# Ordering the block products' preparations on VectorE in one of two feed-forward parts

## The chip, the cores and the metric

The kernel runs on one core of one Trainium2 chip. The metric is device time in microseconds (us), median of several runs; a profiled execution is a run of its own with the hardware profiler on.

## The reference

One decoder layer in float32, x of 512 tokens by 1024 features:

```
x = x + 0.5 * rms_norm(swiglu(rms_norm(x, ffn1_pre), ffn1 weights), ffn1_post)
x = x + rms_norm(token_mixer(rms_norm(x, mix_pre)), mix_post)
x = x + 0.5 * rms_norm(swiglu(rms_norm(x, ffn2_pre), ffn2 weights), ffn2_post)
swiglu(h) = (silu(h @ w_gate) * (h @ w_up)) @ w_down        # w_gate, w_up: 1024 x 2816
```

The token mixer (sparse and dilated attention) stands between the two feed-forward parts and isn't touched.

## The kernel before, in words

**Precision.** Each float32 operand is split into a high half (a cast to fp32r, on ScalarE, line 139) and a low half (source minus high half, on VectorE, line 140). A product then takes three matmuls: high by high, high by low, low by high (`mm3`, lines 162 to 164). For a weight the halves are the tiles whi and wlo, three buffers each. In a product the third matmul is the first that reads wlo. `split` keeps its latest VectorE instruction in `self.last_sub`.

**Block products.** The 2816 hidden features are 22 tiles of 128, taken as 11 pairs p of an even and an odd block. Pairs 0 and 1 are computed plainly. For the pairs 2 to 10 gate and up projections go by a seven-product scheme of the Strassen kind: instead of eight products of block by token half there are seven, P1 to P7, on sums of weight blocks and on sums of token halves made before. Each product has 24 matmuls of 128x128 by 256 tokens, into one bank of PSUM. The seven are run in the order P2, P6, P5, P7, the next pair's P1, P4, P3.

**Preparations.** `prep` makes a product's weight ready: for P6 two sums of raw blocks (lines 509, 510) and one more sum in place (line 524), for P3 one difference in place (line 521), and for every product `entry`, a cast and a subtraction over 128x1024 (lines 139, 140, tiles whi and wlo). P6 and P5 read the sums, tiles tmp; the others read raw blocks. When a raw block is done with, `refill` sends the next load into it through SyncE's queue (line 331; lines 525 and 527 call it). The loop at lines 570 to 581 prepares `AHEAD` = 2 products ahead: in one turn it calls `prep` for the product after next, then `run` for the current one, then `finished`.

**After a product.** `finished` takes results out of PSUM: ScalarE copies (line 544), VectorE adds (lines 548, 553, 560), and `swiglu` (activation on ScalarE at line 402, product on VectorE at line 403; in the first part also a scaling at line 401). Behind P3 `sums` makes sums of the pair's even and odd activations for the down projection, which goes by the same scheme (lines 409 to 412), stores some of them (lines 414 to 419), and for the pairs below `later` splits the even half into fp32r halves at once (lines 423, 424). `later` is 3 in the first part and 11 in the second, so the first part splits there in pairs 0 to 2 and the second in all.

**What sets the order.** A planner puts each engine's instructions in an order when the kernel is built: by its own estimates of time it takes what is ready, the earlier written first, and it may pull later work into a gap. Semaphores and buffers are derived from that. `issue_after(ins)` adds order edges: every instruction that is traced inside the block and belongs to the engine of `ins` is placed behind `ins`. Such an edge is on one engine and needs no semaphore. Around `prep` it is given `self.last_sub`, an instruction of VectorE; so ScalarE's casts and SyncE's refills have no edge of it. `self.last_sub` is whatever split was traced last, be it that of the preparation before or, behind P3, the one in `sums`.

**The two parts.** Both are the function `ffn`. The first is called with `opened`, a dictionary of what the kernel's opening has made; in the second call `opened` is None. The first part also computes weight sums for the down projection by accumulating DMAs (`weight_sums`) during the block products.

Of the kernel before, what the change touches and what calls it, by code (L numbers as in the profile page):

```python
# [61 lines left out]
class Layer:  # L62
# [274 lines left out]
    def ffn(self, gu, wd, td, post, finish, xsrc, aside=None, opened=None):  # L337
# [163 lines left out]
        def prep(p, name):  # L501
            st = state.setdefault(p, {})
            if name == "P1":
                src = blk(p, 0, 0)
            elif name == "P2":
                src = blk(p, 1, 0)
            elif name == "P6":
                s1, s2 = [self.sbt("tmp", [P, D], bufs=2) for _ in range(2)]
                nc.vector.tensor_add(s1, blk(p, 0, 1), blk(p, 1, 1))
                nc.vector.tensor_sub(s2, s1, blk(p, 0, 0))  # L510
                st["s"] = s1, s2
                src = s2
            elif name == "P5":
                src = st["s"][0]
            elif name == "P7":
                src = blk(p, 0, 1)
            elif name == "P4":
                src = blk(p, 1, 1)
            else:
                src = blk(p, 1, 0)  # L520
                nc.vector.tensor_sub(src, src, st["s"][1])
            st[name] = entry(src)
            if name == "P6":
                nc.vector.tensor_sub(blk(p, 0, 1), blk(p, 0, 0), blk(p, 0, 1))
                self.refill(blk(p, 0, 0))
            elif name in ("P7", "P4", "P3"):
                self.refill(src)

        def run(p, name):
            st = state[p]  # L530
            w = st.pop(name)
            bank, top = dict(P1="XB11", P2="YB21", P6="XT2", P5="ZT1", P7="XT3", P4="XT4", P3="ZB22")[name][0:1], \
                dict(P1="B11", P2="B21", P6="T2", P5="T1", P7="T3", P4="T4", P3="B22")[name]
            start = name in ("P1", "P2", "P5")
            if start:
                st[bank] = self.bank()
            product(w, top, st[bank], start)

        def finished(p, name):
            st = state[p]  # L540
            t0, t1 = slice(0, 256), slice(256, 512)
            if name in ("P1", "P6", "P7"):
                v = self.slot("V")
                nc.scalar.copy(v, st["X"])
                st[name + "c"] = v
            if name == "P2":
                v = st["P1c"]
                nc.vector.tensor_add(v, st["Y"], v)
                st["ev"] = self.slot(LATER_TAGS[0][p - later] if p >= later else "ring")
                st["od"] = self.slot("W")  # L550
                swiglu(st["ev"][:, t0], v[:, t0], v[:, t1], t0)
            elif name == "P7":
                nc.vector.tensor_add(v, st["Z"], v)
                swiglu(st["od"][:, t1], v[:, t0], v[:, t1], t1)
            elif name == "P4":
                b = st["X"]
                swiglu(st["od"][:, t0], b[:, t0], b[:, t1], t0)
            elif name == "P3":
                v = st["P6c"]
                nc.vector.tensor_add(v, st["Z"], v)  # L560
                swiglu(st["ev"][:, t1], v[:, t0], v[:, t1], t1)
                sums(p, st["ev"], st["od"])
                extra(p)
                del state[p]
# [4 lines left out]
        done, first = 0, {}  # L569
        for i, (p, name) in enumerate(todo):  # L570
            while done < len(todo) and done <= i + AHEAD:
                with self.tc.issue_after(self.last_sub) if done else ExitStack():
                    prep(*todo[done])
                done += 1
            run(p, name)
            if p == NP - 1 and name in ("P4", "P3"):
                k0 = 2 * len(first)
                r = self.blocks_of.pop(("B11", k0))
                first[k0] = self.wsplit(r.rearrange("p (k d) -> p k d", d=S), [2, S])
                self.refill(r)  # L580
            finished(p, name)
# [1173 lines left out]
```

## Time and profile before

| what | value |
|---|---|
| median of 3 runs | 1138.02 us (1136.74 to 1138.59) |
| the profiled execution's own time | 1144.58 us |
| its span | 1142.8 us |
| TensorE busy | 1106.7 us (97%) |
| VectorE busy | 885.5 us (77%) |
| ScalarE busy | 643.0 us (56%) |
| DMA, mean over the span | 199 GB/s |
| block products of the second part, from and to | 843.5 to 1029.3 us |

How to read it: the profile names engines PE (TensorE matmuls), PEld (its weight loads), DVE (VectorE), ACT (ScalarE), POOL (GpSimd), SP (SyncE). L140 is line 140 of the kernel. A group or a row gives line, engine, operation, and output tile <- input tiles. In a timeline a row begins with its start and its duration in us, and what stands in square brackets is the idle time of the engine before it and the instruction that ended it. Tiles named pb_S, pb_T, pb_F, pb_V are banks of PSUM; xhl_t and SP_s hold the halves of the tokens and of their sums.

### The profile page before, as it was taken

Reading aid. Unit: us, or ns where it says so; the run is one execution under the profiler, and the core shown is the slowest. Engines: PE = TensorE matmul, PEld = TensorE weight load, DVE = VectorE, ACT = ScalarE, POOL = GpSimd, SP = SyncE. Lnnn points to the kernel's source line nnn. Section 1 sums busy time; section 2 is a strip of 40 time slices with the busy share of each in tenths; the row PEclk is TensorE's granted clock in tenths of the full one; section 3 lists DMA queues with packets and bytes.
Section 4 is the critical chain, followed back from the end, with each engine's and each line's share of the span. In section 5 each row is a group of like instructions: output and inputs, shape, how many; then the busy total and the mean of one; then the engine's idle time right before and its main releaser. Section 6 shows DMA issues by size and latency. Waiting matters only on the chain.

```text
span 1142.8 us, 18548 instructions
## 1 busy us (share of the span) xinstructions
PE 1106.7 (97%) x6863; PEld 983.2 (86%) x6863; DVE 885.5 (77%) x1554; ACT 643.0 (56%) x1151; POOL 195.5 (17%) x264
## 2 busy tenths in 40 slices
PE   8999999999999999999999999999999999999997
PEld 7899999977888887777888898888989899887886
DVE  6888999977787889787454656977878989889665
ACT  7454555556574778676564635644435545548452
POOL 0334455420011046553000000001000000000000
PEclk9999999999999999999999999999999999999999
DMA  9699999999973589993224426482234433369863
GB/s 353 208 269 274 295 297 260 292 322 311 319 213 98 183 242 285 276 256 85 82 83 130 133 73 175 139 312 95 77 115 134 130 125 119 122 196 296 292 187 106
DMA packets 115594, 227.53 MB, mean 199 GB/s; under 512 B 21904, under 2 KB 51632, under 8 KB 115504
## 3 DMA queue, kind: packets, MB, share of 16 engines
q1 hardware_dynamic: 99136, 174.18, 46.7%
q0 software_dynamic: 16224, 51.91, 18.2%
q8 instruction: 54, 0.88, 0.3%
q14 instruction: 36, 0.29, 0.1%
q10 hardware_dynamic: 144, 0.26, 0.1%
HBM read 191.66 MB, written 57.72 MB: 218 GB/s over the span
## 4 chain that ended last, share of the span: by engine, by line
PE 72%; DVE 10%; DMA 8%; ACT 4%; issue 4%; POOL 1%; SPq 1%; DVEq 0%; POOLq 0%; ACTq 0%
PE pb_F L164 8%; PE pb_F L163 8%; PE pb_F L162 8%; PE pb_S L164 7%; PE pb_S L163 7%; PE pb_S L162 7%; PE pb_T L164 5%; PE pb_T L163 5%; PE pb_T L162 5%; DMA tdram<-in_d_dram 4%; DVE wlo L140 3%; PE pb_V L162 2%; PE pb_V L163 2%; PE pb_V L164 2%; DMA SP_s<-odram 2%
## 5 line engine op out<-in xcount | busy, mean ns | idle before, releaser
L140 DVE TENSOR_TENSOR wlo<-raw,whi 128x1024 fp32r<-128x1024 f32 (+2 forms) x224 | 264.5, 1186 | 142.1 <-ACT whi L139 137.5
L139 ACT CAST whi<-raw 128x1024 fp32r<-128x1024 f32 (+2 forms) x224 | 228.0, 1020 | 201.9 <-PE pb_F L163 57.0
L162 PE MATMUL pb_F<-xhl_t,whi 128*128 128x512 f32 (+1 forms) x440 | 155.4, 353 | 2.0 <-DVE Q_s L1387 1.2
L164 PE MATMUL pb_F<-xhl_t,wlo 128*128 128x512 f32 (+1 forms) x440 | 154.4, 351 | 0.5 <-DVE wlo L140 0.5
L163 PE MATMUL pb_F<-xhl_t,whi 128*128 128x512 f32 (+1 forms) x440 | 154.3, 351 | 0.0
L183 POOL TENSOR_TENSOR rs_t<-rs_t,mhalf_t 128x1 f32<-128x1 f32 x20 | 13.2, 659 | 571.6 <-DVE rs_t L179 571.6
L162 PEld LDWEIGHTS pb_F<-xhl_t,whi 128*128 128x128 f32 x440 | 82.8, 188 | 12.4 <-DVE Q_s L1387 1.4
L164 PEld LDWEIGHTS pb_F<-xhl_t,wlo 128*128 128x128 f32 x440 | 83.1, 189 | 10.9 <-DVE wlo L140 1.2
L163 PEld LDWEIGHTS pb_F<-xhl_t,whi 128*128 128x128 f32 x440 | 83.0, 189 | 9.6 <-issue 0.2
L162 PE MATMUL pb_S<-xhl_t,whi 128*128 128x256 f32 (+1 forms) x280 | 84.0, 300 | 1.5 <-ACT whi L139 0.8
L163 PE MATMUL pb_S<-xhl_t,whi 128*128 128x256 f32 (+1 forms) x280 | 83.7, 299 | 0.0
L164 PE MATMUL pb_S<-xhl_t,wlo 128*128 128x256 f32 (+1 forms) x280 | 83.5, 299 | 0.0
L1136 POOL TENSOR_SCALAR SP_s<-SP_s,st_t 128x384 f32<-128x384 f32 (+2 forms) x48 | 48.5, 1080 | 72.5 <-DMA raw<-in_w_in_dram 48.7
L162 PEld LDWEIGHTS pb_S<-xhl_t,whi 128*128 128x128 f32 x280 | 52.6, 188 | 4.1 <-ACT whi L139 1.0
L162 PE MATMUL pb_T<-xhl_t,whi 128*128 128x256 f32 x200 | 55.7, 279 | 0.0
L163 PE MATMUL pb_T<-xhl_t,whi 128*128 128x256 f32 x200 | 55.7, 278 | 0.0
L164 PE MATMUL pb_T<-xhl_t,wlo 128*128 128x256 f32 x200 | 55.7, 278 | 0.0
L164 PEld LDWEIGHTS pb_S<-xhl_t,wlo 128*128 128x128 f32 x280 | 53.0, 189 | 2.2
L163 PEld LDWEIGHTS pb_S<-xhl_t,whi 128*128 128x128 f32 x280 | 52.7, 188 | 2.2
L139 ACT CAST whi<-tmp_t 128x1024 fp32r<-128x1024 f32 x36 | 36.3, 1051 | 27.0 <-DVE tmp_t L510 24.0
L164 PE MATMUL pb_S<-SP_s,wlo 128*128 128x256 f32 x160 | 44.9, 281 | 3.8 <-DVE wlo L140 3.8
L140 DVE TENSOR_TENSOR PT_s<-pb_T,PT_s 128x512 fp32r<-128x512 f32 (+1 forms) x72 | 39.3, 560 | 7.1 <-ACT PT_s L139 6.5
(849 smaller groups left out, 3325.7 us busy)
## 6 DMA issues: line engine op xcount, KB each, us to landing
raw<-in_gu_dram SPq DMA_DIRECT2D x74, 512.0 KB, 4.3
raw<-tdram SPq DMA_DIRECT2D x40, 512.0 KB, 5.2
raw<-in_w_in_dram SPq DMA_DIRECT2D x18, 1024.0 KB, 5.3
PT_s<-in_d_dram POOLq DMA_DIRECT2D x66, 256.0 KB, 6.8
raw<-in_d_dram SPq DMA_DIRECT2D x30, 512.0 KB, 4.8
tdram<-in_d_dram POOLq DMA_DIRECT2D x18, 768.0 KB, 11.3
tdram<-PT_s POOLq DMA_DIRECT2D x44, 256.0 KB, 5.5
odram<-W_s SPq DMA_DIRECT2D x22, 256.0 KB, 4.5
```

What stands on the lines that cost most here:

```text
L139: self.last_cast = self.nc.scalar.copy(dsthi, src).ins
L140: self.last_sub = self.nc.vector.tensor_sub(dstlo, src, dsthi.bitcast(F32)).ins
L162: mm(out, lhi, rhi, start=start, stop=False, skip_group_check=skip)
L163: mm(out, lhi, rlo, start=False, stop=False, skip_group_check=skip)
L164: mm(out, llo, rhi, start=False, stop=stop, skip_group_check=skip)
L183: nc.gpsimd.tensor_tensor(out=r, in0=v, in1=self.mhalf, op=OP.pow)
L1136: self.last_pool = nc.gpsimd.tensor_scalar(pp, pp, st[:, 1, t:t + 1], None, op0=OP.mult).ins
```

## The change

The edge around `prep` is set in the first feed-forward part alone. `opened` is a dictionary there and None in the second part, where from now on every preparation is traced without an edge.

```
         for i, (p, name) in enumerate(todo):
             while done < len(todo) and done <= i + AHEAD:
-                with self.tc.issue_after(self.last_sub) if done else ExitStack():
+                with self.tc.issue_after(self.last_sub) if done and opened else ExitStack():
                     prep(*todo[done])
                 done += 1
             run(p, name)
```

More of the change, by code (lines that the diff above doesn't have):

```diff
@@ L571, in ffn @@
             while done < len(todo) and done <= i + AHEAD:
-                with self.tc.issue_after(self.last_sub) if done else ExitStack():
+                with self.tc.issue_after(self.last_sub) if done and opened else ExitStack():
                     prep(*todo[done])
```

## The prediction

> **What bounds the kernel now.** I read the page first, for the engine that sets the time.
>
> ```profile
> span 1142.8 us, 18548 instructions
> PE 1106.7 (97%) x6863; PEld 983.2 (86%) x6863; DVE 885.5 (77%) x1554; ACT 643.0 (56%) x1151; POOL 195.5 (17%) x264
> ```
>
> TensorE (PE) is the bound nearly everywhere, so a reordering on VectorE (DVE) can pay only where TensorE waits for it. Next comes the view by windows. I laid it over one pair of feature blocks (seven products) in the first feed-forward part and over one in the second; its columns are stretch and length, then busy time and instructions of PE, PEld, DVE, ACT and POOL, the granted clock, the DMA share and GB/s.
>
> ```profile
> 150.05:169.84 19.79, 19.79 (x171) 19.79 (x169) 18.50 (x26) 10.42 (x14) 9.66 (x12) 1.00 0.96 278
> 862.50:883.10 20.60, 19.32 (x171) 19.12 (x170) 18.17 (x24) 10.77 (x15) 0.00 (x0) 1.00 0.43 135
> ```
>
> In the first part TensorE is busy for the whole pair. In the second it idles 1.28 us, at the same clock and with fewer DMAs. The view of waits between 840 and 1030 us names who is waited for (total, times, longest):
>
> ```profile
> PE pb_S L164 <- DVE wlo L140: 3.8, 3, 1.3
> PE pb_F L164 <- DVE wlo L140: 2.6, 2, 1.3
> PE pb_T L164 <- DVE wlo L140: 2.6, 2, 1.3
> PE pb_V L164 <- DVE wlo L140: 1.3, 1, 1.3
> ```
>
> That is eight waits, 3+2+2+1, one for each of the pairs 3 to 10, all for the low half (wlo) that line 140 makes on VectorE. The chain that ended last goes through these subtractions:
>
> ```profile
> 871.06 1.23 DVE wlo L140
> ...
> 994.66 1.23 DVE wlo L140
> ```
>
> Six pairs lie between these two, (994.66 - 871.06)/6 = 20.60 us each. Now one such pair in order of time, TensorE first:
>
> ```profile
> 862.50 0.28 PE L162 MATMUL pb_V<-xhl_t,whi 128*128 128x256 f32 x1
> ...
> 865.22 0.28 PE L162 MATMUL pb_F<-xhl_t,whi 128*128 128x256 f32 x1
> ...
> 870.66 0.28 PE L162 MATMUL pb_S<-SP_s,whi 128*128 128x256 f32 x1
> 870.77 0.28 PE L163 MATMUL pb_S<-SP_s,whi 128*128 128x256 f32 x1
> 872.33 0.38 PE L164 MATMUL pb_S<-SP_s,wlo 128*128 128x256 f32 x1 [1.28 <-DVE wlo L140]
> ```
>
> 862.50 and 865.22 are the starts of P3 and of the next pair's P2: a product of 24 matmuls takes 2.72 us. At 870.66 P5 starts; its third matmul is the first that needs wlo, and it starts 1.56 us behind the second where 0.11 is usual. What VectorE did meanwhile:
>
> ```profile
> 866.48 1.22 DVE L140 TENSOR_TENSOR wlo<-tmp_t,whi 128x1024 fp32r<-128x1024 f32 x1
> 867.61 0.42 DVE L403 TENSOR_TENSOR ring_s<-ring_s,V_s 128x256 f32<-128x256 f32 x1
> 868.07 0.42 DVE L409 TENSOR_TENSOR CB_s<-ring_s,W_s 128x256 f32<-128x256 f32 x1
> ...
> 868.75 0.68 DVE L548 TENSOR_TENSOR V_s<-pb_F,V_s 128x512 f32<-128x512 f32 x1
> ...
> 870.45 0.69 DVE L140 TENSOR_TENSOR KA_s<-ring_s,KA_s 128x512 fp32r<-128x512 f32 x1 [0.23 <-ACT KA_s L139]
> 871.06 1.22 DVE L140 TENSOR_TENSOR wlo<-tmp_t,whi 128x1024 fp32r<-128x1024 f32 x1
> ```
>
> and ScalarE, which casts the high halves:
>
> ```profile
> 864.92 2.00 ACT L139 CAST whi<-tmp_t 128x1024 fp32r<-128x1024 f32 x2 [1.83 <-DVE tmp_t L510]
> 869.80 0.62 ACT L139 CAST KA_s<-ring_s 128x512 fp32r<-128x512 f32 x1 [0.66 <-DVE ring_s L411]
> ```
>
> P6's and P5's casts are over at 866.92. P5's subtraction could start then, but it comes at 871.06, right behind the subtraction into KA_s. That one is the split of the pair's finished even half, line 424, and it sets the name `last_sub`. The next preparation is P5's, and line 572 puts its VectorE work behind `last_sub`. The data don't ask for it. In the first part the pairs from 3 on don't split there (`later` is 3), so nothing like it stands in front of P5:
>
> ```profile
> 180.50 1.22 DVE L140 TENSOR_TENSOR wlo<-tmp_t,whi 128x1024 fp32r<-128x1024 f32 x1
> ...
> 182.24 1.21 DVE L140 TENSOR_TENSOR wlo<-tmp_t,whi 128x1024 fp32r<-128x1024 f32 x1
> ...
> 184.97 0.42 DVE L409 TENSOR_TENSOR CB_s<-x_s,W_s 128x256 f32<-128x256 f32 x1
> 188.92 0.68 DVE L140 TENSOR_TENSOR KB_s<-x_s,KB_s 128x512 fp32r<-128x512 f32 x1
> ```
>
> There both subtractions precede the sums (line 409). The last row also shows what the planner does with unbound work: this split belongs to the down projection, written far behind all products, and was pulled into a gap.
>
> **The change part by part.** No instruction, wait or transfer is added or removed: an order edge between instructions of one engine has no instruction of its own. First part: the same code, 0. Second part: 62 of 63 preparations lose their edge, together 98 of 99 VectorE instructions, eleven a pair (seven subtractions and lines 509, 510, 521, 524).
>
> P5, the eight stalls. Without the edge the planner may put P5's subtraction anywhere behind 866.92. It stands ahead of line 548 in the program and behind the sums, so I expect it between 867.6 and 868.75. Even at 868.75 it ends at 869.97, 0.9 us before TensorE wants it at 870.88. Lines 548, 411, 412 and the split come 1.14 us later; the first feeds the next activation, the split is read in the down projection, which begins at 1023.09 (a row below). So each stall ends: 1.56 - 0.11 for the gap and 0.10 for the matmul behind it, which lasts 0.38 instead of 0.28; that is 1.55 us, which agrees with 20.60 - 7 x 2.72 = 1.56. Eight of them: 12.4 us. P5's preparation issues only a cast and a subtraction, no DMA, so SyncE's queue isn't touched by it.
>
> Does VectorE keep up with 19.04 us a pair? It is busy 18.17 in the row above, so 0.87 is left. Its waits in the pair are for casts that start when a product lets go of a whi buffer, and these shrink when it runs late. The first part kept up with 18.50 in 19.79. I take no loss; both ends come under the rivals.
>
> The other preparations. P6's lines 509, 510 and 524 may go into gaps earlier, and their refills (SyncE, lines 525 and 527) with them. In steady state TensorE doesn't wait for them: P6's subtraction ends at 867.70 and its third matmul comes 0.22 us behind P6's start at 865.22 + 2.72 = 867.94. Gain 0; the loss if one is pushed back is a rival.
>
> The way out of the products. TensorE waits three times more before 1050 us, and the chain reaches there from the last P5:
>
> ```profile
> 1015.25 1.22 DVE wlo L140
> ...
> 1016.81 2.28 DVE wlo L140 x2
> 1019.11 0.79 SPq L331
> ```
>
> ```profile
> 1023.09 0.50 PE L162 MATMUL pb_F<-whi,Q_s 128*128 128x512 f32 x1 [1.06 <-ACT whi L139]
> 1044.41 0.50 PE L163 MATMUL pb_S<-wlo,Q_s 128*128 128x512 f32 x1 [0.19 <-DVE wlo L140]
> 1048.18 0.50 PE L163 MATMUL pb_S<-wlo,KA_s 128*128 128x512 f32 x1 [0.73 <-DVE wlo L140]
> 1021.70:1048.00 26.30, 24.50 (x130) 20.37 (x129) 21.27 (x31) 16.96 (x28) 0.00 (x0) 1.00 0.94 305
> ```
>
> An earlier P5 lets P7 and P4 follow earlier, and the refills behind them. At best all three waits go, 1.06 + 0.19 + 0.73 = 2.0 us. At worst the DMA engines, 0.94 busy here, give nothing earlier and the last 1.55 comes back as a wait. I take a third of the best, 0.6 us, because the transfers look like the tighter end.
>
> Sum: 12.4 + 0.6 = 13.0 us. The profiled execution took 1144.58 (span 1142.8 and 1.78 around it), so it would take 1131.6. The median of the three runs is 6.56 below it; the same difference gives **1125.0 us**, 1.1% less. Its own range is 1122 (14.4 saved and 1.5 of scatter, as the runs span 1136.74 to 1138.59) to 1127.2 (10.85 saved).
>
> **The rivals.**
>
> VectorE becomes the bound. A wlo subtraction lasts 1.22 but the next can start 1.13 us behind it (866.48 to 867.61). That overlap is had only where nothing holds the next one. If none were had, a pair would need 11 x 1.22 + 4 x 0.69 + 8 x 0.42 = 19.5 us, with the widths from the rows above. Saved: 8 x (20.60 - 19.54) = 8.5, or 1129.5 us. For it: more instructions would run back to back, and only 0.87 us is free. Against: the rows show the overlap. The Trainium skill, page "VectorE: DVE Perf Modes", section "The DRAIN you can't avoid", says that the next instruction doesn't start until the pipe is empty. By that rule this rival would be the forecast; the trace disagrees, with 1.13 between starts against 1.22 of duration.
>
> Another subtraction becomes late. P6 has the smallest margin: 868.16 - 867.70 = 0.46 us. One instruction of 1.14 put ahead of it, line 524 or P5's own subtraction, costs 0.68 a pair, 5.4 in all: 7.6 saved with the way out, 1130.4 us. Against it: P6 is ready first and stands first in the program.
>
> TensorE's step. The same product takes longer in the first part, at the same granted clock:
>
> ```profile
> 151.46 0.28 PE L162 MATMUL pb_S<-xhl_t,whi 128*128 128x256 f32 x1
> ...
> 154.29 0.28 PE L162 MATMUL pb_F<-xhl_t,whi 128*128 128x256 f32 x1
> ```
>
> 2.83 against 2.72 us, and I can't tell why. If a second part without stalls fell into that step, seven products lose 0.77 a pair, nine pairs 6.9: 6.1 saved, 1131.9 us. Against it: between 843 and 870 us TensorE runs without a stall at the quick step.
>
> Nothing changes. If the planner thinks that P5's cast is late, it leaves the subtraction behind the split: 1138 us. For it: the planner goes by its own costs. Against it: the cast is 4.1 us early.
>
> Slower: VectorE waits for a refill. Line 509 of the next pair reads a block whose load goes out when P7's subtraction is over:
>
> ```profile
> 872.53 2.35 DVE L140 TENSOR_TENSOR wlo<-raw,whi 128x1024 fp32r<-128x1024 f32 x2
> 876.15 1.23 DVE L140 TENSOR_TENSOR wlo<-raw,whi 128x1024 fp32r<-128x1024 f32 x1 [1.26 <-ACT whi L139]
> 873.81 3.92 SPq L331 DMA_DIRECT2D raw<-in_gu_dram  x2
> DMA to landing us min/median/max: 3.3/3.5/5.1
> ```
>
> If the planner puts line 509 into the gap at 874.88, VectorE is held until 873.81 + 3.5 = 877.3, at worst 878.9: 2.4 to 4.0 us, with P4's and P3's subtractions behind it, and TensorE behind those. It decides from 20.60 - 18.17 = 2.43 us on. At 3.2 a pair takes 21.4, eight pairs 6.2 more: 1144 us. Against it: the planner would have to expect the block over 2 us too early.
>
> **How the numbers follow.** Forecast 0.55, VectorE's bound 0.10, another late subtraction 0.08, TensorE's step 0.05, nothing 0.10, slower 0.12. About 0.2%, 2.3 us, is what a measurement of this kernel can tell from no change; the first four cases are faster by more, 0.78. The range goes from the forecast's low end, 1122, over the three smaller gains up to 1137, which leaves out most of "nothing" and all of "slower", 0.2.
>
> **What would show it.** Right: the eight waits of L164 for wlo are gone, starts of P5 lie 19.04 us apart, and on VectorE the second wlo<-tmp_t of a pair stands ahead of the split's row. The rivals show as a new repeated wait of PE for another product's wlo, as starts 19.5 apart with VectorE never idle, as products of 2.83 us, or as line 509 waiting for in_gu_dram. The forecast is wrong if P5's row still follows the split, or if a wait of over 1.5 us a pair stands elsewhere.

## The result, and the profile after

| | before | after |
|---|---|---|
| median of 5 executions | 1138.02 us (1136.17 to 1139.24) | 1129.07 us (1125.24 to 1132.47) |
| the profiled execution | 1144.58 us | 1125.24 us |

The ratio is 0.991 with an interval of 0.9885 to 0.9936: 8.95 us less, by the interval 7.3 to 13.1. The two profiled executions lie 19.3 us apart. That difference is not the change's alone, and the first thing to do is to split it.

All 6863 matmuls run in the same order in both traces, so each can be laid beside itself. After's stand 7.7 us ahead when the second part's block products begin, where the two kernels have done the same work. Of this, 2.3 us comes from the opening, and most of the rest is in these rows. They are one operation's group in the window 75 to 231 us, the first part's block products, with the durations in ns as minimum, median and maximum; before first, then after.

```profile
L164 PE MATMUL pb_S<-xhl_t,wlo x88: 281/281/281, 92.3 to 219.2; 128*128 128x256 f32 x88
```

```profile
L164 PE MATMUL pb_S<-xhl_t,wlo x96: 276/276/276, 89.9 to 227.3; 128*128 128x256 f32 x96
```

(The window catches one product of 8 such matmuls more of the quicker one.) The code is the same, the matmuls are the same, and yet each lasted 281 ns in the one execution and 276 in the other. In starts this is the 2.83 and the 2.72 us a product that the prediction quoted: 117.8 and 113.3 ns a matmul, called the long and the short step below. Before's profiled execution had its first part at the long step, 156.5 us for that stage against 151.3 after. It stood 6.6 us above its median; how much of this the long step makes isn't shown, as its other executions left no trace.

So the change is read in the second part alone. The page of after:

```profile
span 1123.5 us, 18548 instructions
PE 1097.6 (98%) x6863; PEld 975.8 (87%) x6863; DVE 882.0 (79%) x1554; ACT 640.3 (57%) x1151; POOL 195.0 (17%) x264
```

The view of waits, 830 to 1020 us, after:

```profile
ACT W_s L402 <- DVE V_s L553: 23.2, 9, 3.2
...
DVE tmp_t L509 <- DMA raw<-in_gu_dram: 12.1, 8, 2.2
...
PE pb_F L162 <- ACT whi L139: 1.0, 1, 1.0
...
PEld pb_F L164 <- DVE wlo L140: 0.6, 2, 0.3
...
PEld pb_S L164 <- DVE wlo L140: 0.2, 1, 0.2
```

The eight waits of TensorE for wlo, 1.3 us each, are gone. Three of 0.2 to 0.3 us have come, and they show only on the weight loads (PEld). The one of 1.0 us is at the entry to the down projection and was there before (1.06). New is a line of VectorE: line 509 waits eight times for a load. Both can be seen in order of time on VectorE, after:

```profile
895.51 1.22 DVE L140 TENSOR_TENSOR wlo<-tmp_t,whi 128x1024 fp32r<-128x1024 f32 x1
...
897.58 1.21 DVE L140 TENSOR_TENSOR wlo<-tmp_t,whi 128x1024 fp32r<-128x1024 f32 x1
898.71 0.42 DVE L403 TENSOR_TENSOR ring_s<-ring_s,V_s 128x256 f32<-128x256 f32 x1
899.17 0.43 DVE L409 TENSOR_TENSOR PT_s<-ring_s,W_s 128x256 f32<-128x256 f32 x1
...
902.25 0.68 DVE L140 TENSOR_TENSOR KB_s<-ring_s,KB_s 128x512 fp32r<-128x512 f32 x1
...
905.98 1.23 DVE L509 TENSOR_TENSOR tmp_t<-raw 128x1024 f32<-128x1024 f32 x1 [1.57 <-DMA raw<-in_gu_dram]
907.12 1.22 DVE L140 TENSOR_TENSOR wlo<-raw,whi 128x1024 fp32r<-128x1024 f32 x1
...
911.13 1.22 DVE L140 TENSOR_TENSOR wlo<-raw,whi 128x1024 fp32r<-128x1024 f32 x1
```

and on TensorE:

```profile
901.24 0.28 PE L164 MATMUL pb_F<-SP_s,wlo 128*128 128x256 f32 x1
```

```profile
911.89 0.28 PE L162 MATMUL pb_F<-xhl_t,whi 128*128 128x256 f32 x1
912.00 0.28 PE L163 MATMUL pb_F<-xhl_t,whi 128*128 128x256 f32 x1
912.40 0.38 PE L164 MATMUL pb_F<-xhl_t,wlo 128*128 128x256 f32 x1
912.62 0.28 PE L162 MATMUL pb_F<-xhl_t,whi 128*128 128x256 f32 x1
912.74 0.28 PE L163 MATMUL pb_F<-xhl_t,whi 128*128 128x256 f32 x1
912.85 0.28 PE L164 MATMUL pb_F<-xhl_t,wlo 128*128 128x256 f32 x1
```

The second row of VectorE is P5's subtraction. It stands ahead of the sums (line 409) and of the split (KB_s) and ends at 898.79, 2.45 us before the matmul at 901.24 that reads it. The row of line 509 is the cost of the free order: it belongs to the next pair's P6, was pulled ahead of P4's subtraction (907.12), and holds VectorE for 1.57 us until its block has landed. The last row is P3's subtraction. It ends at 912.35, and P3's third matmul starts at 912.40, 0.40 us behind the second where 0.11 is usual. The three rows behind it show more: from 912.62 to 912.74 is 0.12, and it goes on like this. TensorE has gone over to the long step. The view by windows of after (stretch and length, then busy time and instructions of PE, PEld, DVE, ACT and POOL, granted clock, DMA share, GB/s), one row from a P3 to the next P3:

```profile
854.77:873.81 19.04, 19.04 (x170) 19.04 (x169) 17.34 (x24) 10.37 (x15) 0.00 (x0) 1.00 0.41 134
892.85:911.89 19.04, 19.04 (x170) 19.04 (x169) 17.40 (x23) 10.07 (x16) 0.00 (x0) 1.00 0.40 127
911.89:932.05 20.16, 20.04 (x170) 19.85 (x169) 18.63 (x26) 11.29 (x17) 0.00 (x0) 1.00 0.42 134
932.05:951.84 19.79, 19.79 (x171) 19.79 (x169) 17.47 (x23) 10.14 (x15) 0.00 (x0) 1.00 0.39 119
951.84:970.94 19.10, 19.10 (x171) 19.10 (x169) 17.57 (x24) 10.24 (x16) 0.00 (x0) 1.00 0.44 131
```

19.04 is 168 matmuls at 113.3 ns, 19.79 is 168 at 117.8: the fourth row has no wait at all and still costs 0.75 us more, at a granted clock of 1.00 as in the others. At 952.1 a weight load that came some 35 ns late brought the short step back.

Counting each matmul's start to the next start, every trace of this stage (pair 2's P1 to pair 10's P7; pair 10's P4 and P3 belong to the way out) is accounted for to 0.1 us by 165.8 us, plus 4.45 ns for each matmul at the long step, plus TensorE's waits:

| kernel | stage, us | long steps (of some 1460) | waits, us |
|---|---|---|---|
| before | 178.29 | 13 | 12.43 |
| the change, five traces | 168.41, 167.76, 172.31, 168.75, 167.30 | 340, 14, 1463, 455, 12 | 1.08, 1.87, 0.00, 0.92, 1.42 |
| edge among preparations only, three traces | 165.81, 172.31, 165.81 | 1, 1463, 1 | 0.00, 0.00, 0.00 |
| edge for P6 only | 166.06 | 10 | 0.19 |
| all but P6 in order | 169.84 | 790 | 0.52 |
| edge for P5 only | 174.40 | 180 | 7.75 |
| no edge in either part | 172.31 | 1463 | 0.00 |
| preparations only, both parts | 165.81 | 1 | 0.00 |

The way out of the products, TensorE after, answers the three rows of the prediction:

```profile
1005.43 0.73 PE L162 MATMUL pb_F<-whi,Q_s 128*128 128x512 f32 x2 [1.02 <-ACT whi L139]
```

```profile
1026.23 0.39 PE L163 MATMUL pb_S<-wlo,Q_s 128*128 128x512 f32 x1
```

```profile
1028.95 0.39 PE L163 MATMUL pb_S<-wlo,KA_s 128*128 128x512 f32 x1
```

The first wait stays; the second and third have gone. From 1005.43 to 1028.95 are 23.52 us, where the same matmuls lay 25.09 apart before (1023.09 to 1048.18).

### The profile page after: what moved, and what is told of

Same layout as the page of the kernel before. It is cut to its first block, busy times and chain, and to the rows that moved or that the text cites. A ratio compares the mean times of both kernels' runs of the same rounds, so it can differ in the third digit from the quotient of the medians.

```text
span 1123.5 us, 18548 instructions
## 1 busy us (share of the span) xinstructions
PE 1097.6 (98%) x6863; PEld 975.8 (87%) x6863; DVE 882.0 (79%) x1554; ACT 640.3 (57%) x1151; POOL 195.0 (17%) x264
## 4 chain that ended last, share of the span: by engine, by line
PE 49%; DVE 12%; DMA 8%; ACT 5%; issue 4%; POOL 2%; SPq 0%; DVEq 0%; POOLq 0%; ACTq 0%
PE pb_F L164 7%; PE pb_F L162 7%; PE pb_F L163 7%; DVE wlo L140 4%; PE pb_S L163 4%; PE pb_S L164 4%; PE pb_S L162 4%; PE pb_T L162 3%; PE pb_T L163 3%; PE pb_T L164 3%; DMA tdram<-in_d_dram 2%; PE pb_V L162 1%; PE pb_V L163 1%; DMA raw<-in_gu_dram 1%; PE pb_V L164 1%
## 5 line engine op out<-in xcount | busy, mean ns | idle before, releaser
L162 PE MATMUL pb_S<-SP_s,whi 128*128 128x256 f32 x160 | 44.4, 277 | 0.0
```

The costliest lines, as they stand in the source:

```text
L162: mm(out, lhi, rhi, start=start, stop=False, skip_group_check=skip)
```

## The experiments

Two theories of what sets the size stood against each other at first. One: a free order is what helps, since VectorE then takes what is ready. The other: only the tie to the sums' split did harm, and the order among the preparations is worth keeping, because without it line 509 comes too early. A third came up with the traces: TensorE's step decides more than the new waits.

**The preparations in order, but not behind the split.** In the second part the edge is tied to the latest subtraction of a preparation.

```
-                with self.tc.issue_after(self.last_sub) if done and opened else ExitStack():
-                    prep(*todo[done])
+                with self.tc.issue_after(self.last_sub if opened else self.last_prep) if done else ExitStack():
+                    prep(*todo[done]); self.last_prep = self.last_sub
```

> In the second part each preparation is ordered behind the subtraction of the preparation before it, never behind the split of the even half. So of the removed edges only the eight that put P5 behind that split are gone. If these eight edges are the whole cause, the eight waits of TensorE for P5's wlo (1.55 us each, 12.4 in all) are gone, line 509 keeps its place behind P2's subtraction and doesn't wait for a load, and the kernel takes 1123 to 1127 us, the changed kernel or up to 4 us less. If the gain comes from the free placing of all preparations, it loses most of it and takes 1134 us or more.

1123.88 us (1122.18 to 1129.10, 6 executions), ratio 0.9882 (0.9852 to 0.9911). VectorE:

```profile
900.29 1.22 DVE L140 TENSOR_TENSOR wlo<-raw,whi 128x1024 fp32r<-128x1024 f32 x1
...
902.70 1.22 DVE L140 TENSOR_TENSOR wlo<-raw,whi 128x1024 fp32r<-128x1024 f32 x1
904.21 1.23 DVE L140 TENSOR_TENSOR wlo<-raw,whi 128x1024 fp32r<-128x1024 f32 x1 [0.29 <-ACT whi L139]
...
909.65 1.23 DVE L140 TENSOR_TENSOR wlo<-raw,whi 128x1024 fp32r<-128x1024 f32 x1 [0.34 <-ACT whi L139]
910.79 1.22 DVE L509 TENSOR_TENSOR tmp_t<-raw 128x1024 f32<-128x1024 f32 x1
```

Line 509 now comes behind the subtractions of the pair, at 910.79 instead of 905.98, and finds its block there. P4's subtraction stands at 904.21 instead of 907.12 (the stage itself began 0.74 us earlier in this trace). TensorE waits for nothing in the stage: 165.81 us. So moving P5's edge alone away from the split ends all eight stalls, and the order among the preparations costs TensorE nothing in the second part.

**The changed kernel again.**

> The changed kernel once more, for its scatter and a second trace. If its scatter of 7 us comes from the step of TensorE's matmuls (113 or 118 ns for 256 columns), the block products of its second part hold another share of slow steps than the first trace (337 of some 1480), and their length follows that share: 168.5 us less 1.5 for those 337, plus 4.5 ns for each slow one. If it comes from line 509's wait for its load, the waits of TensorE for P3's wlo grow with that wait instead. Time 1125 to 1132 us.

1129.75 us (1123.91 to 1132.30, 6), ratio 0.9917 (0.9887 to 0.9947). Line 509 waits as before (11.1 us in eight), and there are five waits for P3's wlo of 0.15 to 0.39 us. The result repeats, and so do the new waits.

**The edge for P6 only.** Lines 509, 510 and 524 stay where they were; the other six products are free.

```
-                with self.tc.issue_after(self.last_sub) if done and opened else ExitStack():
+                with self.tc.issue_after(self.last_sub) if done and (opened or todo[done][1] == "P6") else ExitStack():
```

> Like the changed kernel, but P6's preparation (lines 509, 510, 524) keeps its edge in the second part. If the early line 509 with its waits for loads (12.1 us on VectorE in the changed kernel) is what makes P3's subtraction late, TensorE's three small waits for it (1.05 us in all) are gone and the kernel is 1 to 3 us faster than the changed one and scatters less. If those waits don't matter, it takes the same time within 1 us.

1126.73 us (1122.18 to 1128.93, 6), ratio 0.9892 (0.9864 to 0.9920). Line 509 doesn't wait, and TensorE waits for 0.19 us in all, in pieces of 0.02 to 0.04. Line 509's waits come from freeing P6, then; that TensorE's new waits do too fits this trace, but they differ much from trace to trace (0 to 1.87 us in the five of the change).

**The edge for P5 only.** The one edge that the prediction held responsible is put back alone.

```
-                with self.tc.issue_after(self.last_sub) if done and opened else ExitStack():
+                with self.tc.issue_after(self.last_sub) if done and (opened or todo[done][1] == "P5") else ExitStack():
```

> The opposite of the first: in the second part P5's preparations alone keep the edge, so they stay behind the split of the even half, and all others are free. If those edges are the cause, TensorE waits 1.2 us or more for P5's wlo in each of eight pairs again and the time is 1135 to 1140 us, the kernel before. If freeing the others is what pays, it stays near 1129 us.

1133.87 us (1129.85 to 1135.47, 10), ratio 0.9957 (0.9938 to 0.9976). The waits:

```profile
PE pb_S L164 <- DVE wlo L140: 1.9, 3, 0.7
...
PE pb_F L164 <- DVE wlo L140: 1.6, 2, 0.9
PE pb_T L164 <- DVE wlo L140: 1.3, 2, 0.9
...
PE pb_V L164 <- DVE wlo L140: 0.8, 1, 0.8
```

All eight are back, which ties them to this edge, but they are smaller: by starts 0.57 to 1.07 us each in place of 1.45, and 7.75 in all with the longer matmul behind each (0.11). The time lies between the two that were expected. One of them on VectorE and on TensorE:

```profile
900.99 0.69 DVE L140 TENSOR_TENSOR KB_s<-ring_s,KB_s 128x512 fp32r<-128x512 f32 x1
901.59 1.22 DVE L140 TENSOR_TENSOR wlo<-tmp_t,whi 128x1024 fp32r<-128x1024 f32 x1
```

```profile
901.79 0.28 PE L162 MATMUL pb_F<-SP_s,whi 128*128 128x256 f32 x1
...
902.86 0.38 PE L164 MATMUL pb_F<-SP_s,wlo 128*128 128x256 f32 x1 [0.69 <-DVE wlo L140]
```

P5's subtraction is right behind the split again, but it begins 0.20 us ahead of P5 itself; before, it was 0.40 behind (871.06 against 870.66). So some 4.7 of the 12.4 us go away without touching P5's edge, by freeing the other products, and all of them by moving P5's edge alone. The edge costs 12.4 us only together with the order of the others, which the prediction had not told apart.

**All but P6 in order.** The mirror image: the kernel with the preparations in order, P6's alone set free.

```
-                with self.tc.issue_after(self.last_sub) if done and opened else ExitStack():
-                    prep(*todo[done])
+                with self.tc.issue_after(self.last_sub if opened else self.last_prep) if done and (opened or todo[done][1] != "P6") else ExitStack():
+                    prep(*todo[done]); self.last_prep = self.last_sub
```

> Like the kernel with the order among preparations alone (1123.88 us, no wait of TensorE in the block products), but P6's preparation is free in the second part, and nothing else. If the early line 509 explains why the changed kernel is some 5 us behind that one, VectorE waits here for loads at line 509 again (over 8 us in all), TensorE has small waits for wlo, and the time is 1126 to 1131 us. If it takes 1125 us or less, line 509's wait is harmless and the 5 us lie elsewhere.

1130.13 us (1127.29 to 1133.84, 6), ratio 0.9926 (0.9906 to 0.9946). Line 509 waits for 11.9 us again. TensorE waited only 0.52 us, but 790 matmuls ran at the long step, 3.5 us. P6's sums alone bring line 509's waits; what they cost in this trace was mostly the step, of which the trace doesn't show that they caused it.

**The preparations in order in both parts.**

```
-                with self.tc.issue_after(self.last_sub) if done and opened else ExitStack():
-                    prep(*todo[done])
+                with self.tc.issue_after(self.last_prep) if done else ExitStack():
+                    prep(*todo[done]); self.last_prep = self.last_sub
```

> The order among preparations alone in both parts. In the first part only pair 2 has an edge behind a split, so at most one stall can go there: 0 to 2 us less than with it in the second part alone, 1121 to 1126 us. If the free place of that one subtraction upsets the first pair's order, it is 1 to 3 us slower.

1129.29 us (1124.50 to 1132.05, 6), ratio 0.9915 (0.9893 to 0.9937): no better than the changed kernel, and not the 1121 to 1126 us that was expected. In its first part the waits did go (0.03 us in place of 4.8), but 1198 matmuls of that stage ran at the long step, 5.3 us, so that it took 151.6 us like the others. The stage between the two block stages took 617.4 us where it takes 610 to 614 in all the other traces; the cause of that stays open.

**The changed kernel a third time**, beside these.

> The changed kernel a third time, for a trace of a further execution. By the two before, line 509 waits 11 to 13 us for loads in all and TensorE 1.0 to 1.9 us for P3's wlo. If that chance alone makes the scatter, block products of 168 us go with about 1124 us, and an execution near 1129 us has block products of 171 us or more, by waits or by slow steps.

1127.81 us (1127.34 to 1132.88, 4), ratio 0.9913 (0.9890 to 0.9937). This trace changes the reading. Line 509 waited as ever (10.3 us), but TensorE didn't wait for wlo; it was itself at the long step from beginning to end. Its group, 835 to 1010 us, and then the same for the first trace of the kernel with the preparations in order:

```profile
L162 PE MATMUL pb_S<-xhl_t,whi x96: 281/281/281, 868.4 to 995.3; 128*128 128x256 f32 x96
```

```profile
L162 PE MATMUL pb_S<-xhl_t,whi x96: 276/276/276, 867.6 to 989.7; 128*128 128x256 f32 x96
```

All at 281 ns and none at 276: 6.5 us more than the short step, the whole of the stage's loss. Nothing was late for TensorE there, so there was no wait left that another order on VectorE could have ended.

**No edge in either part.**

```
-                with self.tc.issue_after(self.last_sub) if done and opened else ExitStack():
+                with ExitStack():
```

> No edge around the preparations in either part. In the first part the DMA engines are 0.96 busy, so if the early line 509 is harmful where loads are late, VectorE waits there for more than the 1.5 us a pair of the second part, TensorE waits for it, and the kernel takes over 1135 us, the gain of the change and more. If the free order is harmless there too, it takes 1127 to 1131 us.

1144.68 us (1138.93 to 1147.18, 7), ratio 1.0044 (1.0024 to 1.0064): slower than before, and 16.9 us slower than the changed kernel beside it. VectorE and the waits in the first part:

```profile
157.98 1.23 DVE L509 TENSOR_TENSOR tmp_t<-CP_s 128x1024 f32<-128x1024 f32 x1 [2.30 <-DMA CP_s<-in_gu_dram]
...
179.79 1.23 DVE L509 TENSOR_TENSOR tmp_t<-raw 128x1024 f32<-128x1024 f32 x1 [2.58 <-DMA raw<-in_gu_dram]
```

```profile
DVE tmp_t L509 <- DMA raw<-in_gu_dram: 8.4, 4, 3.8
...
PE pb_S L164 <- DVE wlo L140: 2.3, 2, 1.2
...
PE pb_F L164 <- DVE wlo L140: 1.4, 2, 1.1
...
PE pb_V L164 <- DVE wlo L140: 1.1, 1, 1.1
PE pb_T L164 <- DVE wlo L140: 1.0, 1, 1.0
```

Here the same line waits up to 3.8 us for a load, and TensorE waits behind it by 0.9 us and more at a time. The stage has 13.0 us of TensorE waits in place of 4.9 and takes 160.9 us in place of 151.1. That trace is of the fastest of the seven executions, 11.1 us above the changed kernel's trace beside it (1138.93 against 1127.85), and this stage makes 9.8 of them; what the slower executions add isn't shown. The rows fit the prediction's mechanism for "slower", in the part whose DMA engines are busy for 0.96 of the time and whose loads are late. No run frees P6 alone in this part, so that line 509 makes all of it stays argued.

**Each of the two again, twice, side by side.** By the first comparison the kernel with the preparations in order was 5.9 us ahead of the changed one. Since one step of TensorE can make 6.5 us, this was tried again.

> The order among preparations alone, once more. So far the block products' length in every trace is 165.8 us plus 4.45 ns for each slow step plus the waits. If that holds, this trace has no wait and a length of 165.8 plus 4.45 ns for each of its slow steps. If its lead of 5 us over the changed kernel was that of the order, its median is 1122 to 1126 us and at least 2 us below the changed kernel's in this comparison; if it was the luck of the step, the two medians are within 2 us.

> The changed kernel beside it: waits of TensorE of 0 to 2 us in the block products, length 165.8 us plus these plus 4.45 ns for each slow step. Median 1127 to 1131 us.

> As order_prep_2. With nothing to interrupt TensorE the step that the block products begin with should last to their end: either all of some 1460 steps slow (172.3 us) or next to none (165.8 us), not a mixture.

> As after_4. Where TensorE waits for P3's wlo the step may change, so mixtures can occur.

Preparations in order: 1127.21 us (1124.59 to 1134.37, 6), ratio 0.9887 (0.9848 to 0.9927), and 1127.59 (1122.51 to 1134.85, 6), 0.9890 (0.9849 to 0.9930). The changed kernel: 1130.55 (1128.44 to 1134.79, 8), 0.9923 (0.9893 to 0.9953), and 1128.91 (1125.28 to 1130.54, 6), 0.9891 (0.9859 to 0.9922). The lead is now 1.3 to 3.3 us, and the intervals overlap. One trace of the kernel in order had all 1463 matmuls of the second part at the long step, the other 1198 of the first part:

```profile
L162 PE MATMUL pb_S<-xhl_t,whi x97: 281/281/393, 834.7 to 996.2; 128*128 128x256 f32 x96, 128*128 128x512 f32 x1
```

So a kernel in which TensorE waits for nothing has the long step too. Over all executions the medians are 1129.49 us (29) for the change and 1126.34 (18) with the preparations in order. It was ahead in all three comparisons (5.9, 3.3 and 1.3 us), by some 3 us over all; the edge for P6 only, at 1126.73, is as fast. How much of the first lead was the step's doing can't be told, because most executions left no trace.

## Why the prediction was right in its main step, and where its sizes were off

The forecast was 13.0 us less, and 8.95 was measured. The time alone proves little: 1129.07 lies outside the forecast's own range (1122 to 1127.2) and within 0.5 us of the 1129.5 of a rival, VectorE as the bound. The traces decide between them: they show the sign that was named, eight waits gone and P5's subtraction ahead of the split. But by its own words the forecast was also to be wrong with "a wait of over 1.5 us a pair" elsewhere, and line 509's 12.1 us in eight are 1.51; this wait stands on VectorE, and TensorE's waits beside it are 1.06 us for the whole stage on average. The mean of the stage over the five traces of the change gives the sum again, term by term:

- The eight stalls, 12.4: right. Before lost 12.43 us in them, and none of the eight is left. P5's subtraction came even earlier than was thought, ahead of the sums. That it was the tie to the split follows from the kernel with the preparations in order, where moving that edge alone ends all the stalls. The edge needs the order of the others for the full price: put back alone, it cost 7.75.
- "The other preparations ... gain 0": this step was mis-sized. P6's lines 509, 510 and 524 did go earlier, but into a wait for the refill, and not P6 but P3 became late. TensorE lost 1.06 us on average (1.08, 1.87, 0.00, 0.92, 1.42). The rival "VectorE waits for a refill" had the mechanism, place and line right. Line 509 was held 1.57 us in the pair shown and 12.1 in eight, against the 2.43 from which it was to decide, so it cost a little and didn't turn the sign. In the first part, where the loads are later, it did.
- "VectorE keeps up": right. The pairs with no wait take 19.04 us, less than the 19.5 that the eleven, four and eight instructions would need without overlap; the row at 907.12 starts 1.14 behind one that lasts 1.23. This rival is refuted here. The rule that the prediction quotes from the Trainium skill (page "VectorE: DVE Perf Modes", section "The DRAIN you can't avoid") has an exception in the same section, "A next op that is not held starts earlier", and these starts of 1.14 us agree with the exception.
- The way out, 0.6: too small. From the stage's last matmul to the third of its waits, the stretch shrank by 1.49 us on average. The transfers were not the tighter end: two of the three waits went (in one of the five traces 0.23 us of the second came), and the one that stayed is for a cast.
- TensorE's step, a rival with a chance of 0.05: far too low, and it was set up as all or nothing. It came in whole (1463 matmuls), in part (340, 455) or hardly (12, 14), 2.0 us on average above before's 13. The prediction's price was right: 0.77 us a pair, against 168 steps of 4.45 ns more, 0.75. This is the largest of the errors. The argument that TensorE ran "without a stall at the quick step" between 843 and 870 us was no evidence against it, because a stage can as well enter at the other step and stay there.
- "Nothing changes": refuted by the row at 897.58.

12.43 - 1.06 - 1.97 + 1.49 = 10.9 us, inside the interval of the result (7.3 to 13.1). The 13.0 lies at the edge of that interval, and it came so near because two errors partly cancel: 3.0 left out, and the way out 0.9 too small. The five comparisons of the change average 0.9913, or 9.9 us. How many of before's executions run at which step in either part is not known, with one trace of it, and the last 1 to 2 us stay open for that reason.

The forecast takes its 13.0 us from the median of the kernel before, 6.56 us below the profiled execution. That was right, because such a distance belongs to one execution: the change's own profiled execution lies 3.8 us below its median. The long step in the first part made some 5.2 us between the two traces, but it isn't shown to be why before's stood above its median. The last trace of the kernel with the preparations in order had 1198 matmuls of that stage at the long step, and its execution, 1127.55 us, stood at the median of its runs, 1127.59.

## What to carry to other kernels

An order edge tied to "the last one traced" catches whatever is traced there; tie it to the kind of work whose order matters. Dropping it altogether was a gain here only where loads were early: the same free order saved some 9 us in the part with half the DMA traffic and cost 16.9 in the other, where the planner pulled a reader of a load ahead of its data. And before two traces are subtracted, lay the same instructions beside each other in a stage that the change doesn't touch: here 7.7 of 19.3 us were not the change's.

## What the runs showed of the hardware that was not expected

The same stream of matmuls of 128x128 by 256 columns with a weight load for each runs at one of two steps, 113.3 or 117.8 ns from start to start (276 or 281 ns long), at a granted clock of 1.00 in both. Within a stage the step changed only where the stream was interrupted, be it by 35 ns (952.1 us) or by 0.28 us (912.0), and in either direction. Without interruption it lasted: 172 us at the long step in one trace of the changed kernel, 166 at the short one in another kernel. All eight waits of 1.45 us in the kernel before ended at the short one. So a stall that is taken away also takes away an occasion to change. Executions of the kernel with the preparations in order, in whose three traces TensorE never waits there, lie between 1122.18 and 1134.85 us; that they scatter more than before's isn't shown. What selects the step was not found. In the Trainium skill, page "TensorE: Matmul & The Clock Gate", section "Back-to-back issue gap", a matmul alone has N/2.4 + 2.5 ns at the full clock, by which 109 ns for 256 columns is an estimate; both steps lie above it, and no run here shows 109.
